# Slots of the split weights 2080 bytes long in place of 2048, in a two-layer encoder trunk

## The chip, the cores and the metric

The kernel runs on one core of one Trainium2 chip. The metric is the time of one execution on the device, in microseconds. It is one launch, with all inputs in the chip's memory (HBM) at the start and the output there at the end.

## What is computed

Two residual layers of an encoder over 512 tokens of width 1024, in float32. Cut to what matters here:

```python
for i in range(DEPTH):                       # 2
    h = rms_norm(x, mix_norm[i])
    x = x + (even_mixer(h, w_in_e, ..., w_out_e) if i % 2 == 0      # sparse attention beside RWKV-7
             else odd_mixer(h, c_w_up, ..., c_w_down))              # mLSTM
    x = x + swiglu_ffn(x, ffn_norm[i], ffn_w_gate[i], ffn_w_up[i], ffn_w_down[i])   # hidden 2816
    x = x + per_layer_embedding(x, p[i], ple_w[i], ple_norm[i], ple_w_gate[i])
```

Nearly all arithmetic is in the projections: `h @ w` with a weight matrix that comes from HBM.

## The kernel before

Everything is kept transposed: a tile has 128 channels as partitions and the 512 tokens along the free axis (`[128, 512]`, 2048 bytes a partition).

**Precision by splitting.** A projection is made of matmuls of the rounded type float32r. To keep float32's accuracy, each operand is split into a rounded part and the rest: `hi = round(x)`, `lo = x - hi`. One block of 128 input channels then takes three matmuls of 128x512: `hi·xhi`, `hi·xlo` and `lo·xhi`. All sum in one PSUM bank.

**Weights.** `weights(src, n)` (line 177) brings four blocks of 128x128 at a time, 256 KB: a DMA on SP's queue into one of four `wraw` buffers, ACT rounds them into a `whi` slot (line 183), and DVE writes the rest into a `wlo` slot (line 184; in two stages GpSimd does that, by `wlo_engine`). `whi` and `wlo` have three slots each (pool `wsplit`, `bufs=3`). `project` (line 207) calls `weights` once for four blocks and issues the 12 matmuls of the four; the call `self.mm` of line 146 is the one that the profile names. So L146 with `whi` or `wlo` in the operands is the projection's matmul, L183 and L184 the split of the weights. A weight block of a slot is its stationary operand (loaded into the array by LDWEIGHTS, engine PEld in the profile), the tokens are the moving one.

**Tokens.** The moving operands (`x`, `h`, `y`, `ya`, `yb`, `p` in the profile, each split into two tiles) stand in slots of 2048 bytes of the pools `arena` (69 slots) and `more` (18), handed out by `take` and `give` from a queue.

**Places in SBUF.** The pools stand one behind the other in each partition: const, wraw, wsplit, small, arena, and then even or more. In the built program the `wraw` buffers begin at bytes 22848, 24896, 26944, 28992, the six slots of `wsplit` at 31040, 33088, 35136 (`whi`) and 37184, 39232, 41280 (`wlo`), `small` at 43328, and the arena at 46400. All of these numbers leave 64 when divided by 256, and so does every arena slot, since a slot is 2048 bytes long.

**First stage.** `first` (line 369) doesn't use `wsplit`: its weights are split into arena tiles `w`, by lines 401 and 402, and its matmuls stand on lines 407 to 409. One of its three matrices is 68 columns wide, so its four blocks of a tile begin 272 bytes apart, at remainders 64, 80, 96 and 112 by 256, in turn for the blocks k = 0, 1, 2, 3 and again for 4 to 7. The other two are 128 wide: their blocks begin 512 bytes apart, all at remainder 64.

**Other matmuls** that are spoken of: line 538 and 541 (float32, not split; `gate` has both operands at remainder 64, `bonus` has a moving operand at 64 and a constant `hblk` at 224 as the stationary one), and `gates` of line 1207, small matmuls of the up-projection of the second layer between its projections.

Of the kernel before, what the change touches and what calls it, by code (L numbers as in the profile page):

```python
# [10 lines left out]
F32R = mybir.dt.float32r  # L11
# [7 lines left out]
P = 128  # L19
S = 512  # L20
# [29 lines left out]
class Trunk:  # L50
# [126 lines left out]
    def weights(self, src, n):  # L177
        nc = self.nc
        raw = self.wraw.tile([P, n], F32, name="wraw", tag="wraw")
        nc.sync.dma_start(raw, src)  # L180
        hi = self.wsp.tile([P, n], F32R, name="whi", tag="whi")
        lo = self.wsp.tile([P, n], F32R, name="wlo", tag="wlo")
        nc.scalar.copy(hi, raw)  # L183
        self.wlo_engine.tensor_tensor(lo, raw, hi.bitcast(F32), op=OP.subtract)  # L184
        return hi, lo
# [1430 lines left out]
```

## Time and profile before

| | |
|---|---|
| median of 3 runs | 1607.37 us (1605.06 to 1609.96) |
| the profiled execution | 1611.13 us |
| its span, first to last instruction | 1609.4 us |
| TensorE (PE) busy | 96% of the span |
| DVE, ACT, POOL busy | 58%, 42%, 19% |
| mean granted TensorE clock | 0.98 of full |

TensorE works nearly the whole span; the other engines prepare its operands and take its results. Matmuls are pipelined: the duration of one, some 0.39 us, is from its start to its modelled end, and the next one starts well before that. How fast TensorE works is therefore read from start to start in the timeline, or from a long unbroken link of the chain divided by its count.

### The profile page before, as it was taken

To read this page: it belongs to the slowest core of one execution; us is meant where nothing else is said; L and a number is where in the kernel's file an instruction comes from. 1 tells how busy PE (TensorE), PEld (TensorE's weight loads), DVE (VectorE), ACT (ScalarE), POOL (GpSimd) and SP (SyncE) were. 2 spreads that over 40 slices of the span, in tenths; PEclk is the share of its full clock that TensorE was granted. 3 is DMA by queue.
4 is the path that set the end of the run, shared out by engine and by line. 5 is a ranking of instruction groups with operands and counts; after the bars stand their busy time and mean duration, and the time that the engine had idled before them with its cause. 6 is when DMAs were issued, how large, how long until landed. Compare 5 with 4: busy or idle time off the path is not lost.

```text
span 1609.4 us, 25291 instructions
## 1 busy us (share of the span) xinstructions
PE 1545.3 (96%) x9811; PEld 1251.8 (78%) x9811; DVE 931.6 (58%) x1721; ACT 677.6 (42%) x1233; POOL 308.7 (19%) x285
## 2 busy tenths in 40 slices
PE   7888989999999999999999999999899999999998
PEld 5666767878888888888777777787788888888887
DVE  6986956566544443336676666657655444443345
ACT  5633445644333333234554655354453333333233
POOL 5563321021000000003300325353420000000002
PEclk9989979999999999999999999999999999999999
DMA  4123220222333333343322113121233333333332
GB/s 160 53 81 96 67 68 16 68 80 92 109 98 99 98 94 107 105 121 125 111 86 86 49 52 104 53 72 48 65 107 96 95 97 98 99 93 98 98 99 99
DMA packets 90112, 142.46 MB, mean 89 GB/s; under 512 B 19588, under 2 KB 24708, under 8 KB 89992
## 3 DMA queue, kind: packets, MB, share of 16 engines
q1 hardware_dynamic: 89992, 140.84, 28.8%
q8 instruction: 77, 1.26, 0.3%
q14 instruction: 43, 0.35, 0.1%
HBM read 133.26 MB, written 7.54 MB: 87 GB/s over the span
## 4 chain that ended last, share of the span: by engine, by line
PE 82%; DVE 12%; ACT 2%; issue 2%; DMA 1%; POOL 1%; SPq 0%; DVEq 0%; POOLq 0%; ACTq 0%
PE mm L146 68%; DVE t L1401 1%; PE s L146 1%; PE v L1355 1%; PE S L1322 1%; PE S L1323 1%; PE S L1321 1%; PE num L1369 1%; DVE t L603 1%; PE num L1371 1%; PE num L1370 1%; PE po L146 1%; POOL t L1486 1%; PE pt L149 1%; PE pair L146 1%
## 5 line engine op out<-in xcount | busy, mean ns | idle before, releaser
L146 PE MATMUL mm<-x,whi 128*128 128x512 f32 (+1 forms) x2496 | 779.0, 393 | 3.5 <-ACT x L309 3.2
L146 PEld LDWEIGHTS mm<-x,whi 128*128 128x128 f32 x2496 | 467.2, 189 | 105.3 <-issue 4.3
L183 ACT CAST whi<-wraw 128x512 fp32r<-128x512 f32 (+1 forms) x470 | 283.9, 606 | 563.2 <-PE mm L146 499.1
L146 PE MATMUL mm<-x,wlo 128*128 128x512 f32 (+1 forms) x1248 | 488.1, 391 | 3.5 <-POOL wlo L184 3.5
L184 DVE TENSOR_TENSOR wlo<-wraw,whi 128x512 fp32r<-128x512 f32 x352 | 244.4, 695 | 244.0 <-ACT whi L183 243.5
L146 PEld LDWEIGHTS mm<-x,wlo 128*128 128x128 f32 x1248 | 235.8, 189 | 53.9 <-POOL wlo L184 4.9
L184 POOL TENSOR_TENSOR wlo<-wraw,whi 128x512 fp32r<-128x512 f32 (+1 forms) x118 | 155.2, 1321 | 341.9 <-ACT whi L183 338.2
L146 PE MATMUL mm<-h,whi 128*128 128x512 f32 x704 | 216.5, 389 | 0.0
L319 POOL TENSOR_TENSOR t<-t 128x512 f32<-128x512 f32 x42 | 56.7, 1349 | 758.3 <-ACT t L318 758.0
L146 PEld LDWEIGHTS mm<-h,whi 128*128 128x128 f32 x704 | 132.1, 188 | 27.3
L146 PE MATMUL mm<-h,wlo 128*128 128x512 f32 x352 | 136.9, 389 | 0.0
L146 PE MATMUL mm<-y,whi 128*128 128x512 f32 x256 | 82.5, 400 | 2.8 <-DVE t L1412 2.8
L146 PEld LDWEIGHTS mm<-h,wlo 128*128 128x128 f32 x352 | 66.1, 188 | 13.8
L1432 DVE TENSOR_TENSOR t<-mm,t 128x512 f32<-128x512 f32 x44 | 30.4, 691 | 64.8 <-PE mm L146 64.8
L1430 DVE TENSOR_TENSOR t<-mm,t 128x512 f32<-128x512 f32 x44 | 30.4, 691 | 64.1 <-PE mm L146 62.5
L146 PEld LDWEIGHTS mm<-y,whi 128*128 128x128 f32 x256 | 49.0, 193 | 13.2 <-ACT whi L183 3.2
L188 ACT CAST h<-t 128x512 fp32r<-128x512 f32 x44 | 27.3, 620 | 66.1 <-DVE t L1433 66.1
L310 DVE SCALAR_TENSOR_TENSOR x<-t,vecs,x 128x512 fp32r<-128x512 f32 x48 | 39.0, 816 | 20.9 <-ACT x L309 20.9
L146 PE MATMUL mm<-y,wlo 128*128 128x512 f32 x128 | 50.8, 397 | 0.0
L189 DVE TENSOR_TENSOR h<-t,h 128x512 fp32r<-128x512 f32 x44 | 30.5, 692 | 29.3 <-ACT h L188 29.2
L309 ACT ACTIVATE x<-t,vecs 128x512 fp32r<-128x512 f32 x48 | 34.8, 724 | 28.3 <-POOL t L1486 15.4
L1216 DVE SCALAR_TENSOR_TENSOR t<-t,vecs 128x511 f32<-128x511 f32 (+2 forms) x48 | 35.7, 749 | 6.1 <-ACT t L1214 5.2
(363 smaller groups left out, 1855.3 us busy)
## 6 DMA issues: line engine op xcount, KB each, us to landing
wraw<-in_ffn_w_gate_dram SPq DMA_DIRECT2D x88, 256.0 KB, 2.6
wraw<-in_ffn_w_up_dram SPq DMA_DIRECT2D x88, 256.0 KB, 2.6
wraw<-in_ffn_w_down_dram SPq DMA_DIRECT2D x80, 256.0 KB, 2.6
wraw<-in_c_w_up_dram SPq DMA_DIRECT2D x64, 256.0 KB, 2.6
wraw<-in_w_in_dram SPq DMA_DIRECT2D x38, 256.0 KB, 2.6
wraw<-in_ple_w_gate_dram SPq DMA_DIRECT2D x32, 256.0 KB, 2.7
wraw<-in_c_w_down_dram SPq DMA_DIRECT2D x32, 256.0 KB, 2.7
t<-in_x_dram SPq DMA_DIRECT2D x16, 256.0 KB, 4.1
```

The costliest lines, as they stand in the source:

```text
L146: self.last = self.nc.tensor.matmul(*args, **kw)
L149: self.last = self.nc.tensor.transpose(*args, **kw)
L183: nc.scalar.copy(hi, raw)
L184: self.wlo_engine.tensor_tensor(lo, raw, hi.bitcast(F32), op=OP.subtract)
L188: self.nc.scalar.copy(hi, src)
L189: self.nc.vector.tensor_tensor(lo, src, hi.bitcast(F32), op=OP.subtract)
L309: nc.scalar.activation(hi, self.x[m], AF.Identity, scale=g)
L310: nc.vector.scalar_tensor_tensor(lo, self.x[m], g, hi.bitcast(F32), op0=OP.mult, op1=OP.subtract)
L319: nc.gpsimd.tensor_tensor(self.acc, self.acc, sq, op=OP.add)
L1216: nc.vector.scalar_tensor_tensor(xc[:, k:], xm[:, :-k], self.vec("cw", 16 * (3 - k) + i), xc[:, k:], op0=OP.mult, op1=OP.add)
L1430: nc.vector.tensor_tensor(gt, pg, self.rstd, op=OP.mult)
L1432: nc.vector.tensor_tensor(ut, pu, self.rstd, op=OP.mult)
```

## The change

The tiles of `wsplit` are asked for with S + 8 = 520 columns, 2080 bytes a partition, whatever n is, and cut to the first n columns at once. What is written to them and read from them is the same.

```diff
         raw = self.wraw.tile([P, n], F32, name="wraw", tag="wraw")
         nc.sync.dma_start(raw, src)
-        hi = self.wsp.tile([P, n], F32R, name="whi", tag="whi")
-        lo = self.wsp.tile([P, n], F32R, name="wlo", tag="wlo")
+
+        hi = self.wsp.tile([P, S + 8], F32R, name="whi", tag="whi")[:, :n]
+        lo = self.wsp.tile([P, S + 8], F32R, name="wlo", tag="wlo")[:, :n]
         nc.scalar.copy(hi, raw)
```

Every engine has the same instructions in the same order with the same waits as before, row for row. What differs is addresses, those of `wsplit` and of every pool behind it, which move up by 6 x 32 = 192 bytes:

| | begins before at | remainder by 256 | begins after at | remainder by 256 |
|---|---|---|---|---|
| wraw, four buffers | 22848 and on | 64 | 22848 and on | 64 |
| whi, three slots | 31040, 33088, 35136 | 64, 64, 64 | 31040, 33120, 35200 | 64, 96, 128 |
| wlo, three slots | 37184, 39232, 41280 | 64, 64, 64 | 37280, 39360, 41440 | 160, 192, 224 |
| small | 43328 | 64 | 43520 | 0 |
| arena, all slots | 46400 and on | 64 | 46592 and on | 0 |
| even, then more in its place | 187712 and on | 64 | 187904 and on | 0 |

## Rows read from the trace of the kernel before

**Rows 1.** The page: engines' busy time, and the chain by engine and line.

```profile
PE 1545.3 (96%) x9811; PEld 1251.8 (78%) x9811; DVE 931.6 (58%) x1721; ACT 677.6 (42%) x1233; POOL 308.7 (19%) x285
...
PE 82%; DVE 12%; ACT 2%; issue 2%; DMA 1%; POOL 1%; SPq 0%; DVEq 0%; POOLq 0%; ACTq 0%
```

**Rows 2.** The chain in order of time: start us, length us, engine, tile, line, count.

```profile
381.22 355.65 PE mm L146 x1569
...
844.25 5.69 PE mm L146 x24
...
1209.37 355.68 PE mm L146 x1569
```

**Rows 3.** Matmuls and weight loads by shape: count | busy us, mean ns | idle before.

```profile
L146 PE MATMUL mm<-x,whi 128*128 128x512 f32 x2464 | 773.2, 394 | 3.5 <-ACT x L309 3.2 <-DVE x L310 0.3
L146 PE MATMUL mm<-x,wlo 128*128 128x512 f32 x1232 | 483.6, 392 | 3.5 <-POOL wlo L184 3.5
L146 PE MATMUL mm<-h,whi 128*128 128x512 f32 x704 | 216.5, 389 | 0.0
```

**Rows 4.** Timeline of PE, last projection, 256 columns: start us, length us, count.

```profile
1601.30 0.28 PE L146 MATMUL mm<-x,wlo 128*128 128x256 f32 x1
1601.42 0.40 PE L146 MATMUL mm<-x,whi 128*128 128x256 f32 x2
1601.66 0.28 PE L146 MATMUL mm<-x,wlo 128*128 128x256 f32 x1
```

**Rows 5.** Timeline of PE in the first stage, the wide matrices and the 68-column one.

```profile
13.21 0.39 PE L407 MATMUL mm<-x,w 128*68 128x512 f32 x1
...
13.89 0.39 PE L407 MATMUL mm<-x,w 128*128 128x512 f32 x1
...
15.25 0.40 PE L407 MATMUL mm<-x,w 128*68 128x512 f32 x1
...
15.95 0.40 PE L407 MATMUL mm<-x,w 128*128 128x512 f32 x1
...
19.39 0.40 PE L407 MATMUL mm<-x,w 128*68 128x512 f32 x1
...
20.10 0.40 PE L407 MATMUL mm<-x,w 128*128 128x512 f32 x1
```

**Rows 6.** Timeline of PE, float32 matmuls with stationary operands at two remainders.

```profile
154.07 1.02 PE L538 MATMUL gate<-t 128*128 128x512 f32 x2
154.93 1.02 PE L541 MATMUL bonus<-bonus,hblk 128*128 128x512 f32 x2
155.79 1.02 PE L538 MATMUL gate<-t 128*128 128x512 f32 x2
```

**Rows 7.** Timeline of PE after a break, second layer's up-projection.

```profile
807.29 0.40 PE L146 MATMUL mm<-x,wlo 128*128 128x512 f32 x1
...
807.99 0.39 PE L146 MATMUL mm<-x,wlo 128*128 128x512 f32 x1
...
810.05 0.39 PE L146 MATMUL mm<-x,wlo 128*128 128x512 f32 x1
...
810.73 0.39 PE L146 MATMUL mm<-x,wlo 128*128 128x512 f32 x1
```

**Rows 8.** Groups by shape on the other engines: count | busy us, mean ns | idle before.

```profile
L183 ACT CAST whi<-wraw 128x512 fp32r<-128x512 f32 x438 | 271.0, 620 | 519.0 <-PE mm L146 457.5 <-issue 18.9 <-ACT t L318 16.8
L184 DVE TENSOR_TENSOR wlo<-wraw,whi 128x512 fp32r<-128x512 f32 x336 | 237.6, 708 | 215.4 <-ACT whi L183 215.0
L184 POOL TENSOR_TENSOR wlo<-wraw,whi 128x512 fp32r<-128x512 f32 x102 | 143.2, 1409 | 308.6 <-ACT whi L183 305.1 <-PE mm L146 3.4
```

**Rows 9.** DMA issues that touch the arena: count, KB each, median us to landing.

```profile
t<-in_x_dram SPq DMA_DIRECT2D x16, 256.0 KB, 4.1
...
out_dram<-t SPq DMA_DIRECT2D x2, 128.0 KB, 1.7
```

**Rows 10.** One stretch of 100 us: engines' busy us and counts, granted clock, DMA share, GB/s.

```profile
200.00:300.00 100.00, 89.54 (x2049) 73.28 (x2048) 59.71 (x201) 54.95 (x157) 16.11 (x29) 0.88 0.13 40
```

## Prediction, made before the changed kernel ran

> **What bounds the kernel now.** I read the page's busy times first: TensorE is busy 1545.3 us of the span of 1609.4, and the chain that ended last is 82% TensorE [rows 1]. Then the chain in order of time: two links, the two feed-forward stages, are 355.65 and 355.68 us of one unbroken run of 1569 matmuls each [rows 2]. That is 355.65 / 1569 = 226.7 ns a matmul, with nothing else in between, for 711 us of the span. So what a change of addresses can be worth is read from the pace of matmuls, start to start; a faster ACT or DVE gives nothing there. ACT's rounding of weights sat idle 519.0 us before its work, 457.5 of them waiting for TensorE to be done with a slot [rows 8]: the slots are full and wait for TensorE, not the other way.
>
> The pace has two parts. With 256 columns three matmuls take 1601.66 - 1601.30 = 0.36 us, 120 ns each [rows 4]; with 512 it is 226.7. The other 256 columns cost 106.7 ns, which is 2.4 columns a ns, the upper level of the clock; 2 x 106.7 = 213.3 is streaming, and 226.7 - 213.3 = 13.3 ns a matmul is a **fixed part**, the same at both widths.
>
> **The change part by part.** No instruction, wait or queue position differs, so there is no term for an operation added or removed. What moves is where operands begin. Before, the stationary block, the moving tile, the raw weights and both slots all begin at remainder 64 by 256; after, the moving tiles begin at 0 and the slots at 64, 96, 128, 160, 192 and 224. Four things could feel that.
>
> (1) *TensorE reading a stationary and a moving operand together.* Could there be a clash now, between starts that are alike, that the change removes? If it came with some neighbour's traffic, the pace would vary. It doesn't: both feed-forward stages, 700 us apart, with ACT, DVE and DMA working beside them, give the same 226.7 to 0.03 us in 355 [rows 2]. Where it is slower, it is after a break: in the up-projection three matmuls take 807.99 - 807.29 = 0.70 us just after the small `gates` matmuls, and 810.73 - 810.05 = 0.68 again some ten matmuls later, with the same slots [rows 7]. That is a start-up, not an address; the alignment there is the same as where there is no excess. So only the fixed part could be the clash. For its stationary side the first stage is a test that the kernel makes by itself: its 68-column blocks begin at 64, 80, 96 and 112 with the moving tile at 64 throughout. The block at 96 runs three matmuls in 13.89 - 13.21 = 0.68 us, 226.7 ns each, exactly the pace of equal remainders [rows 5]. The float32 matmuls agree: with the stationary operand at 64 or at 224 two matmuls' passes take 0.86 us, 154.93 - 154.07 and 155.79 - 154.93 [rows 6]. Value taken: 0 ns a matmul, from the block at 96, the nearest row in type, length and difference (the slots differ from the moving tile by multiples of 32, as it does).
>
> Ends of this term: the split weights have 5472 matmuls in all (the three groups of [rows 3], which hold 4400, and smaller ones of the same line). If the fixed part fell to float32's, 0.43 us a pass less 0.427 for streaming, about 2.5 ns, the gain would be 5472 x 10.8 = 59 us. On the other side stand the blocks at 80 and 112: three matmuls in 20.10 - 19.39 = 0.71 and 15.95 - 15.25 = 0.70 us [rows 5], some 8 ns a matmul over the pace. Those begin at an odd multiple of 16. No slot does, before or after: all six are multiples of 32. Half of them (96, 160, 224) are odd multiples of 32, which is the remainder of the block that ran at full pace. If they too cost 8 ns, three slots of six would cost 5472 / 2 x 8 = 22 us.
>
> The Trainium skill's page "TensorE: Matmul & The Clock Gate", section "Back-to-back issue gap", gives 512 / 2.4 + 2.5, about 215.8 ns, for a matmul of 512 columns from start to start. The trace disagrees: 226.7 [rows 2]. If the 10.9 ns between them were a clash of equal starts, the sum would by that page be 5472 x 10.9, an estimate of 60 us of gain; the block at 96 speaks against it. The same page, section "Step-by-step: what each phase is for", says that TensorE has two independent read ports, so that loading weights takes no bandwidth from the running matmul; by that there is no such clash, and the rows at 96 agree.
>
> (2) *ACT, DVE and GpSimd making the slots.* ACT's rounding takes 620 ns, DVE's rest 708, GpSimd's 1409 [rows 8], all with read and write at equal remainders; for other ones no row is as near. A set of 12 matmuls lasts 12 x 226.7 = 2.72 us, and 620 + 1409 = 2.03 us are hidden under it. What hides a slower split is thus TensorE's own run, 0.7 us a set even in the stages where GpSimd makes `wlo`; a tenth more on every split would be 0.2 us, still covered. With the cover gone it would cost what it exceeds. TensorE's waits for GpSimd's `wlo` are 3.5 us in all [rows 3], so from -3.5 to +3.5 us bounds the term; I take 0.
>
> (3) *DMA.* The weights' buffers `wraw` don't move. Arena tiles now begin at 0: the first loads of x and the last store. Loads of x take 4.1 us to land, the last stores 1.7 [rows 9], and only those two ends lie open. Even a tenth of both is 0.6 us, of either sign. I take 0.
>
> (4) *The clock.* It was at its lower level, 1.2 GHz, for part of the recurrent stage (0.88 on average from 200 to 300 us [rows 10]). When it drops can differ by a few us from one execution to the next, as the three runs' 1605.06 to 1609.96 do. This is spread, not a term.
>
> Sum: 0 + 0 + 0. On the profiled execution that is 1611.1 us again; that execution lay 3.8 us, 0.2%, above the median, and against the median the forecast is **1607.4 us**. What a measurement of this kernel can tell from no change is about 0.3%, 4.8 us; bounds (2) to (4) together are about that, which gives 1602.5 to 1612.5.
>
> **The rivals.**
> *A. The fixed part was a clash of equal starts and falls.* For it: everything stood at 64, and the fixed part is five times float32's. Against it: the block at 96 (though it has 68 columns to load and not 128), and the equal pace of both float32 forms. Price 59 us if all of it goes: 1548. A part of it would already show: 1 ns a matmul is 5.5 us.
> *B. Slower: blocks at odd multiples of 32 read like those at odd multiples of 16.* Weight loads from three of the six slots then cost some 8 ns a matmul, 22 us: 1629; if every slot whose remainder differs from the moving tile's costs it, 44 us: 1651. It decides from under 1 ns a matmul on, as nothing hides TensorE's pace in the feed-forward stages. For it: the blocks at 80 and 112 show that the start of a stationary operand can matter at all. Against it: the block at 96, and that the excess at 112 goes on at 64 in the wide blocks that follow, so it may be a disturbance and not a price of the load.
> *C. The change doesn't do what it says.* It says that six slots get six remainders; it does that, but it also shifts the arena, so that the moving tiles' starts change for the float32r matmuls that take no weights from `wsplit`, too. A pace that came from the moving tile's own start would change for all. No row has a moving tile elsewhere than at 64; streaming at 2.4 columns a ns leaves nothing to gain but the fixed part, so its prices are those of A and B.
>
> **How the numbers follow.** No change that can be told: 0.88. A, with C's share: 0.05. B, with C's share: 0.07. So faster by over 0.3% 0.05, within 0.3% 0.88, slower 0.07. The range, 1602.5 to 1612.5, is the likeliest case's own and leaves out the two others, 0.12.
>
> **What would show it.** Right: the two long links of the chain stay at 355.7 us for 1569 matmuls, and the last projection at 0.36 us for three. A would show as shorter links (350 is already 3.6 ns a matmul), alike in both stages. B would show as pairs of projections' runs at two paces, by slot, and links near 365. If (2) is wrong, ACT's or GpSimd's mean for the split rises and TensorE's idle time before `wlo` with it. The forecast is wrong if the links keep their length and the time still moves by over 5 us: then the cause lies in the recurrent stage, its clock, or a DMA.

## The result: slower by 1.1%

The changed kernel took 1625.14 us (median of 4 runs, 1623.01 to 1626.94), the kernel before 1607.22 beside it (4 runs, 1605.06 to 1609.96). The ratio is 1.011, with a 95% interval of 1.0088 to 1.0132. The time is 17.9 us above the kernel before. The forecast was 1607.4 and no change that can be told; the time lies 17.7 us above that and outside the range.

The changed kernel's profiled execution took 1626.64 us with a span of 1624.8, 15.4 us more than before's 1609.4. Its page, the engines' busy times and the chain by engine:

```profile
PE 1563.7 (96%) x9811; PEld 1247.0 (77%) x9811; DVE 931.7 (57%) x1721; ACT 678.4 (42%) x1233; POOL 308.1 (19%) x285
...
PE 83%; DVE 12%; ACT 2%; issue 1%; DMA 1%; POOL 0%; SPq 0%; DVEq 0%; ACTq 0%
```

Against [rows 1], the instruction counts are the same; PE is busy 18.4 us longer, DVE, ACT and POOL differ by at most 0.8. The chain in order of time (start us, length us, engine, tile, line, count):

```profile
377.39 363.42 PE mm L146 x1569
...
848.36 5.78 PE mm L146 x24
...
1216.51 363.46 PE mm L146 x1569
```

Against [rows 2], each of the two feed-forward links is 7.8 us longer for the same 1569 matmuls: 363.42 / 1569 = 231.6 ns a matmul in place of 226.7. The two links together are 15.5 us longer, as much as the whole span. The short run of 24 went from 5.69 to 5.78. The shapes, by count | busy us, mean ns | idle before (the code has one line more from the tiles of `wsplit` on, so that line 184 is now ACT's rounding and 185 the rest):

```profile
L184 ACT CAST whi<-wraw 128x512 fp32r<-128x512 f32 x438 | 270.7, 619 | 541.3 <-PE mm L146 492.5 <-ACT t L319 17.5 <-issue 14.6
L185 DVE TENSOR_TENSOR wlo<-wraw,whi 128x512 fp32r<-128x512 f32 x336 | 236.5, 704 | 222.7 <-ACT whi L184 222.1
L185 POOL TENSOR_TENSOR wlo<-wraw,whi 128x512 fp32r<-128x512 f32 x102 | 142.7, 1403 | 309.3 <-ACT whi L184 309.2
```

Against [rows 8]: 619, 704 and 1403 ns for 620, 708 and 1409. The three engines that write the slots don't feel their remainders. ACT only waits longer for TensorE, 492.5 us in place of 457.5, as its turn comes later. TensorE is idle for 1624.8 - 1563.7 = 61.1 us of the span, where it was 64.1: it doesn't wait longer but does the same matmuls at a slower pace. A timeline of PE inside the first link (start us, length us, count):

```profile
500.24 0.63 PE L146 MATMUL mm<-x,whi 128*128 128x512 f32 x2
500.70 0.40 PE L146 MATMUL mm<-x,wlo 128*128 128x512 f32 x1
500.94 0.62 PE L146 MATMUL mm<-x,whi 128*128 128x512 f32 x2
501.40 0.39 PE L146 MATMUL mm<-x,wlo 128*128 128x512 f32 x1
501.63 0.62 PE L146 MATMUL mm<-x,whi 128*128 128x512 f32 x2
```

Three matmuls take 0.70 and 0.69 us here, where 0.68 was the rule before [rows 7]. In the gate and up projections single starts lie 228 to 236 ns apart once the run is under way, in a pattern that repeats every 36 matmuls, that is, every three sets of slots. No slot stands out: sorted by the slot that a matmul loads from, the means lie between 231.8 and 232.5 ns for the three `whi` and between 230.0 and 231.9 for the three `wlo`.

Outside the links the differences nearly cancel. The windows of both kernels (stretch, length, then busy us and count of PE, PEld, DVE, ACT, POOL, granted clock, DMA share, GB/s) from the start to the first link and between the two links, first before:

```profile
0.00:381.22 381.22, 343.97 (x4054) 268.45 (x4055) 273.32 (x624) 190.55 (x421) 132.10 (x151) 0.94 0.25 78
...
736.87:1209.37 472.50, 450.30 (x2417) 361.68 (x2417) 315.36 (x549) 232.52 (x396) 150.24 (x114) 0.98 0.26 78
```

and after:

```profile
0.00:377.39 377.39, 342.20 (x4054) 264.85 (x4055) 273.36 (x624) 190.76 (x421) 131.70 (x151) 0.96 0.25 79
...
740.81:1216.51 475.70, 454.31 (x2416) 360.29 (x2417) 314.26 (x549) 232.73 (x396) 150.10 (x114) 0.99 0.25 78
```

The front is 3.8 us shorter, at a granted clock of 0.96 for 0.94, and the middle 3.2 us longer. With 0.5 us after the second link the balance is 7.8 + 7.8 - 3.8 + 3.2 + 0.5 = 15.5, the span's 15.4 but for rounding.

### The profile page after: what moved, and what is told of

The parts are those of the page before. It is cut to its first block, busy times and chain, and to the rows that moved or that the text cites. A ratio compares the mean times of both kernels' runs of the same rounds, so it can differ in the third digit from the quotient of the medians.

```text
span 1624.8 us, 25291 instructions
## 1 busy us (share of the span) xinstructions
PE 1563.7 (96%) x9811; PEld 1247.0 (77%) x9811; DVE 931.7 (57%) x1721; ACT 678.4 (42%) x1233; POOL 308.1 (19%) x285
## 4 chain that ended last, share of the span: by engine, by line
PE 83%; DVE 12%; ACT 2%; issue 1%; DMA 1%; POOL 0%; SPq 0%; DVEq 0%; ACTq 0%
PE mm L146 70%; DVE t L1402 1%; PE s L146 1%; DVE t L604 1%; PE num L1370 1%; PE S L1323 1%; PE S L1324 1%; PE S L1322 1%; PE num L1371 1%; PE num L1372 1%; PE pair L146 1%; PE po L146 1%; PE pt L149 1%; DVE big L778 1%; DVE m L603 1%
## 5 line engine op out<-in xcount | busy, mean ns | idle before, releaser
L146 PE MATMUL mm<-x,whi 128*128 128x512 f32 (+1 forms) x2496 | 789.2, 396 | 2.7 <-ACT x L310 2.5
L146 PE MATMUL mm<-h,whi 128*128 128x512 f32 x704 | 220.4, 394 | 0.0
```

Source lines behind the costliest of these rows:

```text
L146: self.last = self.nc.tensor.matmul(*args, **kw)
```

## The experiments

Three theories stood after the comparison, and the expectations below name them by number. Theory 1: blocks that are loaded one after the other from different remainders cost time. Theory 2: what counts is the distance, by 256 bytes, of the stationary block from the moving tile: the block's start less the tile's. Theory 3: the arena's new place, remainder 0, is the cause, and the slots have no part in it. "Distance" is used in that sense from here on. Before, it is 0 for every matmul of the links. In the changed kernel it is 64, 96, 128, 160, 192 or 224, by slot. Each experiment but the last is one execution, so its links are read rather than its time.

**The arena alone.** The slots stay at 64; a spare tile behind them moves the arena to remainder 0, as in the changed kernel.

```diff
+        pool("post", 1).tile([P, 48], F32, name="post")
```

> The six slots stay as before, 2048 bytes each and all at remainder 64; 192 unused bytes behind them move small, arena, even and more to remainder 0, exactly where the changed kernel has them. Theory 1 (what costs is that stationary blocks that follow each other begin at different remainders): the two feed-forward links stay at 355.7 us for 1569 matmuls, the time at 1607. Theory 2 (what costs is the distance between the stationary block's start and the moving tile's): every matmul now has the distance 64 where it had 0, so the links are longer than 355.7 us, near the changed kernel's 363.4 or more, and the time near 1625. Theory 3 (the arena's new place is the whole cause): the links and the time of the changed kernel, 363.4 and 1625.

Measured: 1630.27 us beside 1603.09. Both links are the same:

```profile
375.03 366.10 PE mm L147 x1569
...
1217.57 366.10 PE mm L147 x1569
```

366.10 / 1569 = 233.3 ns a matmul, and uniformly so. All slots share one remainder here, so Theory 1 gives no loss; yet the links are longer than the changed kernel's 363.42.

**The slots alone.** Slots of 2080 bytes, and a spare tile that puts the arena back at remainder 64.

```diff
+        pool("post", 1).tile([P, 16], F32, name="post")
...
-        hi = self.wsp.tile([P, n], F32R, name="whi", tag="whi")
-        lo = self.wsp.tile([P, n], F32R, name="wlo", tag="wlo")
+        hi = self.wsp.tile([P, 520], F32R, name="whi", tag="whi")[:, :n]
+        lo = self.wsp.tile([P, 520], F32R, name="wlo", tag="wlo")[:, :n]
```

> The six slots are 2080 bytes long, at remainders 64, 96, 128, 160, 192 and 224 as in the changed kernel; 64 unused bytes behind them bring small, arena, even and more back to remainder 64. Theory 1 (changing remainders): links near 363.4 us, time near 1625, although the moving tiles stand as before. Theory 2 (distance to the moving tile): the distances are 0, 32, 64, 96, 128 and 160 in place of 64 to 224, so longer than 355.7, but with another mean than 363.4, and the matmuls with the whi slot at 64 keep 226.7 ns. Theory 3 (the arena): 355.7 us and 1607.

Measured: 1624.15 us beside the same 1603.09.

```profile
374.88 363.82 PE mm L147 x1569
...
1213.67 363.81 PE mm L147 x1569
```

231.9 ns a matmul with the arena where it was. Theory 3 falls: each half of the change suffices alone. The slot at distance 0 doesn't run at 226.7 either, which Theory 2 in its simplest form, a price for each matmul by its own slot, wants: in this run's trace no slot's mean is under 230.5 ns.

**All moved together.** A spare tile ahead of the slots puts them and the arena at 128; `wraw` stays at 64.

```diff
+        pool("pre", 1).tile([P, 16], F32, name="pre")
```

> Slots of 2048 bytes; 64 unused bytes ahead of wsplit, so that all slots and the arena begin at remainder 128, and only the raw weights' buffers stay at 64. Theories 1, 2 and 3: the links of the kernel before, 355.7 us, and 1607. If the remainder itself counts (64 is a good start for TensorE and others aren't): longer links. If ACT's and DVE's reading at 64 and writing at 128 counts: longer means for the split of the weights, more than 620 ns on ACT, 708 on DVE and 1409 on GpSimd.

Measured: 1606.95 us beside 1603.09, one run each.

```profile
376.37 355.68 PE mm L147 x1569
...
1205.19 355.68 PE mm L147 x1569
```

The links are those of [rows 2] to 0.03 us. So 128 is as good as 64 when slots and arena share it, and what counts is how they lie to one another. That `wraw` and the slots now differ by 64 costs nothing: the splits take 620, 708 and 1407 ns.

**`whi` with the moving tiles, `wlo` apart.** `wlo` gets a pool of its own at 160, distance 96; `whi` keeps distance 0.

```diff
+        pool("mid", 1).tile([P, 24], F32, name="mid")
+        self.wspl = pool("wsplitlo", 3)
+        pool("post", 1).tile([P, 40], F32, name="post")
...
-        lo = self.wsp.tile([P, n], F32R, name="wlo", tag="wlo")
+        lo = self.wspl.tile([P, n], F32R, name="wlo", tag="wlo")
```

> Slots of 2048 bytes; the three whi slots and the arena at remainder 64, the three wlo slots at 160. So of three matmuls two have a stationary block at the moving tile's remainder, and the remainder changes twice in three matmuls. Theory 1 (changing remainders): links clearly longer than 355.7, toward 363.4. Theory 2 (distance to the moving tile): only the matmuls with wlo, or those during which it is loaded, are slower; the hi matmul that follows a hi one keeps 226.7 ns, so about a third to two thirds of the changed kernel's excess, 358 to 361 us. Theory 3 (the arena): 355.7.

Measured: 1624.64 us beside 1603.09.

```profile
375.07 364.93 PE mm L149 x1569
...
1212.94 364.93 PE mm L149 x1569
```

232.6 ns. Two thirds of the matmuls have distance 0 and are slow all the same: by place and slot, the first of a pair from `whi` takes 232.9 to 233.8 ns in this run's trace, the second 231.1 to 232.2, and the one from `wlo` 232.5 to 233.2. A price by a matmul's own distance is refuted. Theory 1 could still say that the change of remainder costs; against it stands the first experiment.

**A map of distances.** `whi` and `wlo` are written and read at an offset into slots of 2560 bytes (ten times 256). It takes a new value with every second hidden block of the feed-forward stages: 11 values a layer, 96 matmuls each. One `wraw` buffer is given up for the room.

```diff
-        self.wraw = pool("wraw", 4)
+        self.wraw = pool("wraw", 3)
...
+        o = self.at // 4
+        hi = self.wsp.tile([P, S + 128], F32R, name="whi", tag="whi")[:, o:o + n]
+        lo = self.wsp.tile([P, S + 128], F32R, name="wlo", tag="wlo")[:, o:o + n]
...
+            self.at = ((0, 32, 64, 96, 128, 160, 192, 224, 256, 288, 320), (0, 352, 384, 416, 448, 480, 16, 48, 8, 4, 512))[i][j // 2]
```

> Distances measured within one execution: the slots of wsplit are 2560 bytes long, so all six begin at the arena's remainder (by 512 too), and the weights are written at a distance into the slot that changes every two hidden blocks of the feed-forward stages (96 matmuls, some 22 us at one distance): in the first layer 0, 32, 64, 96, 128, 160, 192, 224, 256, 288, 320 bytes, in the second 0, 352, 384, 416, 448, 480, 16, 48, 8, 4, 512 (which is 0 by 512 again). There are three raw buffers in place of four to make room. Theory 2 in its plain form (any distance but 0 costs one step): 226.7 ns a matmul at 0 and 512, 233.3 at 64 and 320 as in arena_only, and 233.3 at all others. Theory 2 with a period of 64 or 128 bytes, or with 32 bytes free, as the first stage's block at 96 says: 226.7 at 32 as well. Theory 2 with a graded price: a value of its own for each distance, perhaps some under 226.7, the fixed part then being itself an address effect. Theory 1 (changing remainders): 226.7 at every distance, with a start-up of ten matmuls after each change.

Measured: 1614.34 us beside 1605.97. A group begins at its first matmul. Windows cut at these starts, columns as above; the distances are 64, 192, 224, 256 and 288:

```profile
411.87:434.27 22.40, 22.40 (x98) 18.05 (x96) 10.51 (x16) 7.50 (x12) 0.00 (x0) 1.00 0.31 96
...
501.45:523.44 21.99, 21.99 (x97) 18.03 (x96) 10.41 (x16) 7.48 (x12) 0.00 (x0) 1.00 0.29 96
523.44:545.83 22.39, 22.39 (x97) 17.99 (x96) 10.50 (x16) 7.48 (x12) 0.00 (x0) 1.00 0.29 94
545.83:567.60 21.77, 21.77 (x97) 18.02 (x96) 10.36 (x16) 7.46 (x12) 0.00 (x0) 1.00 0.30 96
567.60:589.99 22.39, 22.39 (x97) 18.04 (x96) 10.51 (x16) 7.48 (x12) 0.00 (x0) 1.00 0.31 97
```

A length divided by 96 is the pace: 233.3, 229.1, 233.2, 226.8 and 233.2 ns (PE's counts of 97 and 98 take in matmuls that lie across an edge). Clock, DMA and the other engines are alike in all five and the edit changes nothing but the offset between them, so the distance is the cause. In the second layer, 16 and 512:

```profile
1332.61:1354.37 21.76, 21.76 (x97) 18.02 (x96) 10.36 (x16) 7.46 (x12) 0.00 (x0) 1.00 0.30 95
...
1421.22:1443.01 21.79, 21.79 (x97) 18.02 (x96) 10.45 (x16) 7.37 (x12) 0.00 (x0) 1.00 0.33 97
```

They run at 226.7 and 227.0. The distances 32 and 288, 64 and 320, 96 and 352 and so on agree in pairs within 0.2 ns: the period is 256. The others gave 234.2 (96), 232.4 (128), 233.3 (160), 233.3 (48), 230.7 (8) and 232.4 (4).

**The map at steps of 16 and 8.** The same kernel with other values.

```diff
+            self.at = ((80, 112, 144, 176, 208, 240, 24, 40, 56, 72, 88), (104, 120, 136, 152, 168, 184, 200, 216, 232, 248, 12))[i][j // 2]
```

> As sweep, with the distances between: in the first layer's feed-forward stage 80, 112, 144, 176, 208, 240, 24, 40, 56, 72 and 88 bytes, in the second's 104, 120, 136, 152, 168, 184, 200, 216, 232, 248 and 12. If 226.7 ns is the least there is (two streams that are in step): no distance under 226.7, most near 233. If the fixed part of 13.3 ns is an address effect as a whole: some distance well under 226.7, at least near 220, which would make the whole kernel faster by 5000 x 6.7 ns, some 33 us.

Measured: 1619.70 us beside 1607.19. The first row is distance 120, the second 136:

```profile
1226.22:1247.99 21.77, 21.77 (x98) 18.02 (x96) 10.36 (x16) 7.46 (x12) 0.00 (x0) 1.00 0.30 96
1247.99:1270.38 22.39, 22.39 (x98) 18.02 (x96) 10.51 (x16) 7.50 (x12) 0.00 (x0) 1.00 0.29 94
```

226.8 ns at 120, 233.2 at 136. In the steady part of the groups: 233.3 to 233.4 at 40, 56, 72, 88, 104, 112, 136, 144, 168 and 248, 228.3 to 232.3 at the rest but 120, and nothing below 226.7 at any distance. Of all that were tried only 0, 16 and 120 run at 226.7. As no distance tried beats 0, none of these offsets beats the kernel before.

**Two distances at once, and narrow loads.** In the second layer `whi` and `wlo` take an offset each. In the first layer 18 of the 24 matmuls of each gate and up projection, those of the second to seventh of its eight blocks, load 68 columns in place of 128; the sums of the other 60 columns leave these blocks out.

```diff
+        o, ol = (b // 4 for b in self.at)
...
+        lo = self.wsp.tile([P, S + 128], F32R, name="wlo", tag="wlo")[:, ol:ol + n]
...
+                w = 68 if self.narrow and 0 < k < n - 1 else m
```

> Two questions in one execution. In the first layer's feed-forward gate and up projections, 18 of each 24 matmuls load 68 columns and not 128 (the second to seventh block of eight; the outputs of the other 60 columns miss those blocks, so this part is not computed), at the distances 0, 16, 32, 48, 64, 96, 128, 160, 192, 224 and 240. If a narrow load has the same price as a wide one: the values of sweep, 226.7 at 0 and 16, 233 at 32, 48 and 64. If the first stage's rows (226.7 at 32, some 8 ns more at 16 and 48) hold for narrow loads: 226.7 at 32, more at 16 and 48; then the row was read rightly and did not stand for wide loads. In the second layer's stage whi and wlo have distances of their own: (0, 16), (16, 0), (0, 32), (32, 0), (0, 192), (192, 0), (0, 240), (16, 240), (64, 128), (0, 256), (0, 8). Theory 2: (0, 256), (0, 16) and (16, 0) at 226.7, the others above it by a part of their single prices. Theory 1 (changing remainders costs by itself): (0, 16) and (16, 0) above 226.7 as well.

Measured: 1611.99 us beside 1607.19. The pairs (`whi`, `wlo`) of these windows are (16, 0), (32, 0), (0, 240), (16, 240) and (0, 256):

```profile
1219.81:1242.21 22.40, 22.40 (x98) 18.14 (x96) 10.50 (x16) 7.48 (x12) 0.00 (x0) 1.00 0.30 97
1264.59:1286.85 22.26, 22.26 (x98) 18.02 (x96) 10.47 (x16) 7.47 (x12) 0.00 (x0) 1.00 0.31 95
1331.01:1352.77 21.76, 21.76 (x98) 18.02 (x96) 10.36 (x16) 7.46 (x12) 0.00 (x0) 1.00 0.30 98
1352.77:1374.53 21.76, 21.76 (x98) 18.02 (x97) 10.35 (x16) 7.45 (x12) 0.00 (x0) 1.00 0.32 98
1396.72:1418.48 21.76, 21.76 (x97) 18.02 (x96) 10.36 (x16) 7.46 (x12) 0.00 (x0) 1.00 0.30 98
```

(16, 240) changes the remainder with two matmuls of every three and runs at 226.7: a change of remainder costs nothing in itself, and Theory 1 falls. (16, 0) mixes two distances that are free alone and costs the full 6.7 ns. (0, 240) is free, though 240 alone ran at 228.3. So single prices don't add up; the pace belongs to the whole sequence of loads and streams.

The narrow loads have another map again. These are the 12 matmuls in the middle of one projection each, all narrow, at the distances 16, 32 and 48, and then of a gate and of the next up projection, both at 128:

```profile
388.32:391.10 2.78, 2.78 (x13) 1.65 (x12) 2.78 (x8) 1.24 (x2) 0.00 (x0) 1.00 0.26 94
410.45:413.19 2.74, 2.74 (x13) 1.65 (x12) 2.05 (x4) 1.24 (x2) 0.00 (x0) 1.00 0.28 96
438.07:440.86 2.79, 2.79 (x13) 1.66 (x12) 0.93 (x2) 0.78 (x2) 0.00 (x0) 1.00 0.33 94
499.28:502.08 2.80, 2.80 (x14) 1.65 (x12) 2.07 (x4) 1.24 (x2) 0.00 (x0) 1.00 0.25 94
504.85:507.57 2.72, 2.72 (x14) 1.65 (x12) 0.80 (x2) 0.80 (x2) 0.00 (x0) 1.00 0.28 96
```

Divided by 12, narrow loads take some 232 ns at 16, 228 at 32 and 232 at 48, where wide ones take 226.7, 233.3 and 233.3. That is the order of [rows 5]: the block at 96 was read rightly for its own width and doesn't stand for wide loads. At 128 the same matmuls at the same distance take 233.3 ns in the gate projection and 226.7 in the up projection, and so again with the next hidden block; what sets the one or the other, no run shows.

**Half the moving columns.** Gate and up in two halves of 256 columns, 192 matmuls to a distance.

```diff
+        for run in cols or ([slice(0, S // 2), slice(S // 2, S)] if self.half else [slice(0, S)]):
...
+            self.at = ((0, 16, 32, 48, 64, 80, 96, 112, 128, 144, 160), (176, 192, 208, 224, 240, 8, 24, 56, 120, 136, 248))[i][j // 2]
```

> The gate and up projections of both feed-forward stages run as two halves of 256 columns, 48 matmuls in place of 24, at distances that change every two hidden blocks: 0, 16, 32, 48, 64, 80, 96, 112, 128, 144, 160 in the first layer, 176, 192, 208, 224, 240, 8, 24, 56, 120, 136, 248 in the second. In the kernel before a 256-column matmul took 120.0 ns, in arena_only (distance 64) 113.6. If the price of a distance belongs to one load, whatever is streamed beside it: the order of sweep, least at 0, 16 and 120, more at 64. If it depends on how load and stream lie to each other in time: another map than at 512 columns, 113.6 at 64, 120 at 0. If some distance gives 110 ns or less, 256-column matmuls would be faster there than 512-column ones at 226.7.

Measured: 1624.88 us beside 1606.15. The distances of these windows are 32, 64 and 112:

```profile
411.48:434.20 22.72, 22.72 (x195) 22.72 (x193) 10.52 (x17) 7.47 (x12) 0.00 (x0) 1.00 0.29 94
456.81:478.57 21.76, 21.76 (x194) 21.76 (x193) 10.46 (x17) 7.48 (x12) 0.00 (x0) 1.00 0.32 98
523.91:546.95 23.04, 23.04 (x194) 23.04 (x193) 10.55 (x17) 7.47 (x12) 0.00 (x0) 1.00 0.28 92
```

Divided by 192: 118.3, 113.3 and 120.0 ns. With 256 columns distance 64 is the best of the 22 tried and 0 is among the worst (120.0, the pace of [rows 4]); 512 columns have it the other way round. Two halves at their best take 2 x 113.3 ns, some 226.7, one whole at its best as well, so no distance tried makes halving pay.

**Longer slots, same remainder.** `whi` slots of 576 columns, 2304 bytes or nine times 256.

```diff
-        hi = self.wsp.tile([P, n], F32R, name="whi", tag="whi")
+        hi = self.wsp.tile([P, 576], F32R, name="whi", tag="whi")[:, :n]
```

> The three whi slots are 2304 bytes long in place of 2048, so that they begin at three different places by 2048 or by 512, but all at remainder 64 by 256; wlo slots and the arena stay at 64 as well. If the distance by 256 is what counts: links of 355.7 us for 1569 matmuls and the time of the kernel before within 0.3%. If slots have to be 2048 bytes long, or places by 512 or more count: longer links, toward 363, and a time toward 1625.

Measured: 1607.50 us (10 runs) beside 1606.15 (13), ratio 1.0004, 95% interval 0.9994 to 1.0014.

```profile
380.06 355.67 PE mm L146 x1569
...
1208.74 355.67 PE mm L146 x1569
```

Longer slots that shift everything behind them cost nothing, as long as they leave the distances at 0.

## Why the prediction was wrong

**What held.** The pace of TensorE is the bound, the two links are the place to read it, and a change of addresses acts there or nowhere. Terms (2) and (3), the splits and the DMA, were taken at 0 and are 0: 619, 704 and 1403 ns for a split, and the loads of x take 4.3 us to land and the last stores 1.7, against 4.1 and 1.7 [rows 9].

**The step that failed is term (1)**, "Value taken: 0 ns a matmul, from the block at 96". It measured 4.9 ns a matmul in the links, 231.6 less 226.7. The block at 96 [rows 5] ran at distance 32 and at full pace, but for three matmuls between others at distance 0 and with 68 columns to load. In steady work, wide loads at distance 32 take 233.3 ns. Those at distance 16, which [rows 5] shows as slow, run at 226.7: at both distances the row gave the reverse of what steady wide loads do, and only its slow block at 112, distance 48, agrees with them. The width accounts for that: steady narrow loads keep the order of the row, some 228 ns at 32 and 232 at 16 and 48. I had named the difference in width as a weakness and still let the row decide. Nor does any slot of the changed kernel have the distance 32: I compared remainders of slots and left out that the arena had moved to 0. The float32 pair of [rows 6] was no support either: its distance is 160, where steady float32r loads took 233.3 ns.

**The argument from the uniform pace was one-sided.** That the pace before didn't vary showed that nothing varying disturbed it. From that I asked only whether equal starts were a clash that the change would take away. It didn't occur to me that equal starts could be the good case. Every operand of the links stood at the same remainder, so the rows that I had read held no steady run of them at any other distance; that should have widened the range upwards and not counted as evidence for 0.

**Rival B** had the sign and nearly the size: half of the slots at 8 ns a matmul, 22 us, against 17.9 measured. That the size is near is chance, as its mechanism, odd multiples of 32, was wrong: 64 costs as much as 32 and 96, and 128 nearly as much. Its alternative, every slot whose remainder differs pays 8 ns, gave 44 us and is closer in mechanism but too dear: the excess is 6.7 ns at most of the bad distances, and 4.9 in the mixture of six. **Rival C** said that the shift of the arena has the prices of A and B. Its part is real, and by itself larger than the whole: the arena's shift alone cost 27.2 us in one execution, 20.9 of them in the links, where both together cost 15.5, since six slots at one bad distance (233.3 ns) are worse off than six at different ones (231.6).

**The sum.** 5472 x 4.9 ns would be 27 us, and 17.9 came. The links, 3138 matmuls, hold 15.5. In the middle part the span grew by 3.2 us. The front has the loss too, a link of 102 projection matmuls in it going from 23.16 to 23.63 us, but its granted clock was 0.96 in place of 0.94 and it became 3.8 us shorter. Term (4) had this as spread. That front is between 374.88 and 381.22 us long in all kernels shown here with their links, and the four kernels with slow links have it below 377.5; but the kernel at 128, which has the pace of before, has 376.37, at 0.95. Whether a slower pace earns a better clock there stays open.

**What stays open** is the mechanism. The matmul's pace depends on where the block that is loaded begins relative to the tile that is streamed, with a period of 256 bytes. It depends on the number of columns loaded and streamed too, and on the sequence rather than on the matmul alone; for narrow loads at 128 not even distance and shape settle it. The Trainium skill's page "TensorE: Matmul & The Clock Gate", section "Step-by-step: what each phase is for", says that TensorE has two independent read ports, so that loading weights takes no bandwidth from the running matmul. The runs show a limit of that: with nothing but the start of the loaded block changed, the pace goes from 226.7 to 233.3 ns; whether it is bandwidth that is lost, they don't show. The 215.8 ns by the formula of the same page of the Trainium skill, section "Back-to-back issue gap", which the section gives for isolated matmuls, were not reached at any distance. Where the loss arises, no run here shows; moving tiles at two different remainders were not tried.

## What to carry to other kernels

Where float32r matmuls of 512 columns run back to back, each with a load of 128 columns, keep the weights' tiles and the tokens' tiles at the same remainder by 256 bytes: pad slots by whole multiples of 256 (2304 bytes cost nothing, 2080 cost 1.1%), and look where every pool behind a padded one comes to lie. This is not a rule for other shapes: with 256 columns distance 64 was best, so measure the map for the shape at hand. After any change to sizes in SBUF, divide the longest unbroken link of matmuls by its count; if it moved with the same instructions, compare addresses first. A row that tests a question must agree in shape, type and length with what it stands for; here 68 columns to load in place of 128 turned the answer round.

## What the runs showed of the hardware

- A float32r matmul of 128x512 with a load of its own took 226.7 ns at the least over all distances tried; the loss at most bad distances is 6.7 ns, 233.3 less 226.7 before rounding, the time of 16 columns at the prediction's 2.4 columns a ns. With 256 columns the ends are 113.3 and 120.0, 6.7 ns apart again.
- So the 13.3 ns a matmul that the prediction called a fixed part, the same at both widths, is none. At distance 64 the 256-column matmul has 113.3 - 106.7 = 6.7 ns of it, while 512 columns at 64 have 233.3 - 213.3 = 20.
- ACT, DVE and GpSimd, which write the slots, don't feel the remainders: a split of 128x512 takes the same mean time within 1% (619, 704 and 1403 ns for 620, 708 and 1409) with its source and its target 0 to 160 bytes apart by 256.
